# Two widening layers formed by features instead of by tokens, in a two-block transformer kernel

## Chip, core and metric

The kernel runs as one program on one core of a Trainium2 chip. The metric is the device time of one execution in microseconds (us), the median of three runs. Smaller is better. The engines are named as the profile names them: PE is the matrix engine, PEld its weight loads, DVE the vector engine, ACT the scalar engine, POOL the general-purpose engine, SP the queue that issues the large loads.

## The reference, cut to what matters

Two transformer blocks run one after the other on 256 tokens of width 2048, all in float32. The parts that the change touches are the feed-forward networks at the end of each block:

```python
# end of the first block, D_FF = 8192
u = jax.nn.relu(rms_norm(h, mlp_norm_g) @ w_up)
h = h + (u * u) @ w_down
...
# end of the second block, D_FF_2 = 5632
h = rms_norm_2(x, ln_ffn_pre[l])
y = (jax.nn.silu(h @ w_gate[l]) * (h @ w_up[l])) @ w_down[l]
x = x + rms_norm_2(y, ln_ffn_post[l])
```

`rms_norm` divides each token by its root mean square and multiplies by a gain per feature. The widening layers are `w_up` (2048 to 8192) in the first network, `w_gate` and `w_up` (2048 to 5632) in the second.

## The kernel before

**Products in split form.** Each float32 operand is held as a high part, rounded to the type fp32r, and a low part, the rest. A product is three matmuls: high by high, high by low, low by high. Weights come from memory in units of 128 x 1024 floats (two k tiles of 512 columns); ACT writes the high part (`wh`, line 133 by way of line 360), DVE the low part (`wl`, line 366). Five raw buffers and six pairs of `wh` and `wl` are in rotation, and a unit is split up to four units ahead of its use.

**Groups.** `run_groups` (lines 399 to 481) walks a list of groups, each a product of the 256 tokens with 512 output columns. For each k tile of 128 rows it takes the tokens in two halves `t` of 128. The tokens are the stationary operand (128 columns, loaded into the array before each matmul) and 512 weight columns move past them, so that the result has tokens on the partitions and features along the row. One bank of PSUM holds one half; four banks serve two groups in turn. A group with 16 k tiles issues 96 matmuls of 512 columns (lines 460 to 462), and `up` and gate groups have 16 k tiles. A form with the weights stationary and 256 tokens moving exists for the two narrow weights of 20 and 48 columns alone (`swap`, lines 447 to 456).

**What follows a group.** When a group's last matmul is written, its `done` generator becomes a task. `pump` steps the tasks between k tiles, so that their matmuls, transposes and evacuations are placed into the queues between the matmuls of the next groups. The order on every engine is thus written out ahead of time; on the chip an instruction waits only for semaphores and for the one before it on its engine. A planner's clocks (`pe_t`, `act_t`, `dve_t`) decide at which k tile a step is placed.

**The widening layers.** In the first network `up` (line 1065) takes one of 16 groups: ACT applies relu and the token's reciprocal root mean square (`rs`, one number per partition) to each bank, DVE squares the result, and `u_T` transposes it by eight 128 x 128 transposes on PE (line 203, two lots of four) and splits it into high and low parts with ACT and DVE, because the narrowing product needs the features on the partitions. In the second network `ffn_gate` (line 1625) and `ffn_up` (line 1634) do the same for 11 pairs of groups with silu and a product; the eight transposes follow each `ffn_up`. The narrowing groups (`dn`, `fd`) follow two widening groups later, so that `up2` and `up3` come before `dn0_0`.

**The norm.** The gain is applied to the tokens' transposed tiles; the sums of squares are formed by ACT, reduced by DVE, raised to the power -0.5 by POOL (`rstd`, line 232), and the result scales the outputs. In the first network this chain runs in the task of the group `out3`, just as `up0` begins; in the second network it runs during `fg0`.

Of the kernel before, what the change touches and what calls it, by code (L numbers as in the profile page):

```python
# [10 lines left out]
F32 = mybir.dt.float32  # L11
# [79 lines left out]
class Group:  # L91
    def __init__(self, name, w, lhs, done, need=None, n=512, fine=False):
        self.name, self.lhs, self.done, self.need, self.n = name, lhs, done, need or {}, n
        self.bk = {}
        self.task = self.tset = self.tneed = None
        self.per_t = self.resume = self.pause = False
        self.swap = n < 512
        if n == 512:
            srcs = []
            for c in range(w.shape[0]):  # L100
                d = 1 if fine and c == 0 else 2
                srcs += [(w[c][:, j:j + d, :], d, 4 * c + j) for j in range(0, 4, d)]
        else:
            srcs = [(w, 16, 0)]
        self.units = [Unit(self, s, k, n, kt0, i == 0, i == len(srcs) - 1)
                      for i, (s, k, kt0) in enumerate(srcs)]


class Program:
# [289 lines left out]
    def run_groups(self, groups):  # L399
# [27 lines left out]
        for un, ts, ahead in steps:  # L427
            g = un.grp
            if un.first and not g.resume:
                for t in ts:  # L430
                    g.bk[t] = self.bank()
            while self.si < un.i:
                self.split(self.si + 1)
            self.ahead = ahead
            self.more()
            for e in g.need.get(un.kt0 // 4, ()):
                self.need(e if g.tneed is None else (*e, ts[0]))
            lhs = g.lhs()
            h, l = un.pair
            n = un.n  # L440
            self.pe_t = max(self.pe_t, un.ready)
            for k in range(un.nkt):
                kt = un.kt0 + k
                H, L = lhs[0][kt // 4], lhs[1][kt // 4]
                st, sp = un.first and k == 0 and not g.resume, un.last and k == un.nkt - 1 and not g.pause
                wh, wl = h[:, k * n:k * n + n], l[:, k * n:k * n + n]
                if g.swap:
                    c = (kt % 4) * 256
                    o = g.bk[0]["ap"][:n, :256]
                    mm(o, wh, H[:, c:c + 256], start=st, stop=False)  # L450
                    mm(o, wl, H[:, c:c + 256], start=False, stop=False)  # L451
                    mm(o, wh, L[:, c:c + 256], start=False, stop=sp)  # L452
                    self.pe_t += 325.0
                    if k % 4 == 3 and not sp:
                        self.pump()
                    continue
                for t in ts:
                    c = (kt % 4) * 256 + t * 128
                    o = g.bk[t]["ap"]
                    mm(o, H[:, c:c + 128], wh, start=st, stop=False)  # L460
                    mm(o, H[:, c:c + 128], wl, start=False, stop=False)  # L461
                    mm(o, L[:, c:c + 128], wh, start=False, stop=sp)  # L462
                    self.pe_t += 648.0
                if sp:
                    break
                if len(ts) == 2 or k % 2:
                    self.pump()
            if 1 in ts:
                if un.slot is None:
                    self.R.put(*un.pair)  # L470
                else:
                    self.pfree[un.slot] = self.pe_t
                    self.ring.append(un.slot)
            if un.last and not g.pause:
                if g.per_t:
                    self.over(g, g.done(g.bk[ts[0]]["ap"], ts[0]), [g.bk[ts[0]]])
                elif 1 in ts:
                    bs = [g.bk[t] for t in sorted(g.bk)]
                    self.over(g, g.done([b["ap"] for b in bs]), bs)
                self.pump()  # L480
# [96 lines left out]
    def fin_ssq(self, sq, key):  # L577
        s2 = self.stat(2)
        self.red(s2, sq, OP.add)
        self.rs[key] = self.rstd(s2, 2, 2048.0)  # L580
        self.ev.add(("rs", key))

    def free_TT(self, key):
        for x in self.TT.pop(key):
# [3 lines left out]
def v3(f, a):  # L588
    return f.rearrange("p (a b) -> p a b", a=a)


class Kernel(Program):
# [470 lines left out]
        yield from self.norm_T(f, c, "h", "mlp_norm_g", self.sq_h)  # L1063

    def up(self, banks, j):
        yield from self.until(("rs", "h"))
        rs = self.rs["h"]
        (f,) = yield from self.F.wait()
        f3 = v3(f, 2)
        for t in range(2):  # L1070
            self.act(f3[:, t], banks[t], AF.Relu, scale=rs[:, t:t + 1])
        if j == 15:
            self.free_TT("h")
        yield "B"
        self.tt(f, f, f, OP.mult)
        yield 1
        yield from self.u_T(f3, j, 2)
        self.F.put(f)

    def u_T(self, f3, j, per):  # L1080
        h, l = yield from self.R.wait(2)
        yield from self.T_split(f3, None, h, l)
        H, L = self.TT.setdefault(("u", j // per), ([None] * per, [None] * per))
        H[j % per], L[j % per] = h, l
        self.ev.add(("u", j))

    def down(self, banks, b, c):
# [546 lines left out]
    def ffn_up(self, banks, j):  # L1634
# [13 lines left out]
        H[k], L[k] = h, l  # L1648
        self.ev.add(("w", j))

    def ffn_down(self, banks, b, c):
        if b == 0:
            (f,) = yield from self.F.wait()
            self.S["y", c] = f
            for t in range(2):
                self.copy(v3(f, 2)[:, t], banks[t])
            yield "B"
        else:
            f = self.S["y", c]
            f3 = v3(f, 2)  # L1660
            for t in range(2):
                self.tt(f3[:, t], banks[t], f3[:, t], OP.add)
            yield "B"
        if c == 3:
            self.free_TT(("w", b))
# [92 lines left out]

    def build(self):
        nc, A = self.nc, self.A  # L1760
        self.rs, self.S, self.nsq = {}, {}, {}
        self.TT = {"o": ([None] * 4, [None] * 4), "a": ([], []), "p": ([], [])}
        self.gla_e = self.gla_n = 0
        self.KEEP = 6
# [89 lines left out]
        for c in range(4):  # L1854
            G.append(g("out%d" % c, A["w_out"][c], "o", lambda b, c=c: self.wout(b, c), L("oT")))

        ups = [g("up%d" % j, A["w_up"][j], "h", lambda b, j=j: self.up(b, j), L("h") if j == 0 else None)
               for j in range(16)]

        def downs(b):  # L1860
# [4 lines left out]
        def inter(up, dn, nb, per):  # L1865
# [3 lines left out]
                seq += dn(b)  # L1869
            return seq  # L1870

        mlp = inter(lambda b: ups[2 * b:2 * b + 2], downs, 8, 2)
        G += mlp

# [60 lines left out]
        def gu(b):  # L1935
            r = []
            for j in range(2 * b, min(2 * b + 2, 11)):
                r.append(g("fg%d" % j, A["w_gate"][j], "hf", lambda k, j=j: self.ffn_gate(k, j),
                           L("hf") if j == 0 else None))
                r.append(g("fu%d" % j, A["w_up_2"][j], "hf", lambda k, j=j: self.ffn_up(k, j)))  # L1940
            return r

        def fd(b):
# [4 lines left out]

        ffn = inter(gu, fd, 6, 2)
        ffn[0].tset, ffn[0].tneed = "fg0", True  # L1950
        for x in ffn[-4:]:
            x.tset, x.per_t = "fd5", True
        G += ffn
# [193 lines left out]
```

## Time and profile before

| what | value |
|---|---|
| median of three runs | 2643.56 us (2643.45 to 2644.34) |
| profiled execution's own time | 2642.02 us |
| its span, first to last instruction | 2640.3 us |
| PE busy | 2616.5 us (99% of the span), 12196 matmuls |
| PEld busy | 2168.9 us (82%) |
| DVE busy | 1504.9 us (57%) |
| ACT busy | 1251.9 us (47%) |
| POOL busy | 76.5 us (3%) |
| granted PE clock, mean | 0.998 of full speed |
| loads of weights | 473.16 MB on the SP queue |

Busy time of a group of instructions is the union of their durations. A matmul's recorded duration is longer than the distance from its start to the next one's start, since matmuls are pipelined; the speed of a stream is read from starts. The three large groups of the page are the matmuls of lines 460, 461 and 462, each 3496 times, and the chain that ended last runs for 94% of the span through PE.

### The profile page before, as it was taken

How to read it: one execution, taken by the hardware profiler on the slowest of the kernel's cores; microseconds unless marked ns; L12 is line 12 of the kernel's file. 1: busy time of each engine (PE TensorE's matmuls, PEld its weight loads, DVE VectorE, ACT ScalarE, POOL GpSimd, SP SyncE). 2: the span in 40 equal slices, each digit the busy share in tenths (PEclk: the TensorE clock that was granted, in tenths of full speed). 3: DMA queues.
4: the chain of work that ended last, by engine and by line, in shares of the span. 5: the costliest groups of instructions: out<-in, count | busy, mean ns of one | idle time of the engine just before them, and what ended most of it. 6: DMA issues, size and time to landing. Idle time of an engine off the chain costs nothing.

```text
span 2640.3 us, 32053 instructions
## 1 busy us (share of the span) xinstructions
PE 2616.5 (99%) x12196; PEld 2168.9 (82%) x12196; DVE 1504.9 (57%) x1921; ACT 1251.9 (47%) x1708; POOL 76.5 (3%) x97
## 2 busy tenths in 40 slices
PE   9999999999999999999999999999999999999998
PEld 7888888888888888888888888888788888888886
DVE  6567655555555555555566545666755455555555
ACT  7544544444444444444455344465554444444443
POOL 0001000000000000001000000000100000000001
PEclk9999999999999999999999999999999999999999
DMA  9643565555566565555444557555455555556553
GB/s 343 204 139 119 166 216 185 188 188 184 191 201 223 187 223 195 191 202 198 150 143 147 190 177 258 201 199 184 136 193 189 192 188 194 186 195 202 195 186 129
DMA packets 138891, 500.18 MB, mean 189 GB/s; under 512 B 15650, under 2 KB 16594, under 8 KB 138737
## 3 DMA queue, kind: packets, MB, share of 16 engines
q1 hardware_dynamic: 131760, 473.16, 53.0%
q0 software_dynamic: 6976, 24.98, 2.7%
q8 instruction: 95, 1.56, 0.2%
q14 instruction: 60, 0.48, 0.1%
HBM read 493.33 MB, written 7.88 MB: 190 GB/s over the span
## 4 chain that ended last, share of the span: by engine, by line
PE 94%; issue 4%; DVE 1%; ACT 0%; DMA 0%; POOL 0%; SPq 0%; DVEq 0%; ACTq 0%; POOLq 0%
PE gb L460 29%; PE gb L462 29%; PE gb L461 29%; PE pb L197 4%; PE pb L203 3%; DVE wl L366 0%; DVE s L169 0%; DMA s<-memT 0%; DVE s L158 0%; POOL st L232 0%; ACT wh L133 0%; PE gb L451 0%; ACT s L133 0%; PE gb L450 0%; PE gb L452 0%
## 5 line engine op out<-in xcount | busy, mean ns | idle before, releaser
L366 DVE TENSOR_TENSOR wl<-raw,wh 128x1024 fp32r<-128x1024 f32 (+1 forms) x876 | 1052.8, 1219 | 689.5 <-ACT wh L133 687.4
L460 PE MATMUL gb<-wh,s 128*128 128x512 f32 x3496 | 1383.9, 396 | 2.2 <-ACT wh L133 2.1
L461 PE MATMUL gb<-wl,s 128*128 128x512 f32 x3496 | 1362.5, 390 | 2.5 <-DVE wl L366 2.5
L462 PE MATMUL gb<-wh,s 128*128 128x512 f32 x3496 | 1363.4, 390 | 0.0
L133 ACT ACTIVATE wh<-raw 128x1024 fp32r<-128x1024 f32 (+1 forms) x878 | 914.0, 1055 | 802.2 <-PE gb L462 766.8
L462 PEld LDWEIGHTS gb<-wh,s 128*128 128x128 f32 x3496 | 656.4, 188 | 139.3 <-DVE s L169 0.5
L460 PEld LDWEIGHTS gb<-wh,s 128*128 128x128 f32 x3496 | 657.2, 188 | 137.4 <-ACT wh L133 3.7
L461 PEld LDWEIGHTS gb<-wl,s 128*128 128x128 f32 x3496 | 657.5, 188 | 135.1 <-DVE wl L366 4.2
L158 DVE TENSOR_TENSOR s<-gb,s 128x512 f32<-128x512 f32 x144 | 98.1, 691 | 159.6 <-PE gb L462 130.5
L133 ACT ACTIVATE s<-pb 128x512 fp32r<-128x512 f32 (+4 forms) x171 | 89.4, 536 | 163.6 <-PE pb L203 139.5
L133 ACT ACTIVATE s<-gb,st 128x512 f32<-128x512 f32 (+1 forms) x112 | 70.0, 642 | 199.5 <-PE gb L462 188.0
L197 PE MATMUL pb<-s,s 128*128 128x128 f32 (+4 forms) x720 | 116.5, 301 | 1.3 <-DVE s L158 0.9
L203 PE MATMUL pb<-cc,s 128*128 128x128 f32 x700 | 106.0, 274 | 5.4 <-DVE s L169 5.3
L203 PEld LDWEIGHTS pb<-cc,s 128*128 128x128 f32 x700 | 87.0, 141 | 29.0 <-DVE s L169 6.6
L197 PEld LDWEIGHTS pb<-s,s 128*128 128x128 f32 x720 | 97.7, 191 | 9.5 <-DVE s L158 1.3
L158 DVE TENSOR_TENSOR s<-pb,s 128x512 fp32r<-128x512 f32 (+4 forms) x87 | 57.5, 664 | 62.4 <-ACT s L133 58.6
L133 ACT ACTIVATE s<-pb,vecs 128x256 fp32r<-128x256 f32 (+2 forms) x109 | 42.3, 453 | 49.9 <-PE pb L203 40.5
L163 DVE TENSOR_SCALAR s<-gb,st 128x512 f32<-128x512 f32 (+1 forms) x32 | 20.9, 658 | 67.8 <-PE gb L462 51.5
L169 DVE SCALAR_TENSOR_TENSOR s<-pb,vecs,s 128x256 fp32r<-128x256 f32 (+1 forms) x104 | 40.0, 435 | 29.0 <-ACT s L133 29.0
L133 ACT ACTIVATE s<-s,st 128x128 f32<-128x128 f32 (+2 forms) x73 | 32.8, 450 | 31.7 <-DVE st L163 30.4
L133 ACT ACTIVATE s<-s 128x512 f32<-128x512 f32 (+3 forms) x46 | 37.0, 807 | 21.5 <-DVE s L158 12.4
L232 POOL TENSOR_TENSOR st<-st,nhalf 128x8 f32<-128x8 f32 (+2 forms) x21 | 26.1, 1243 | 689.5 <-DVE st L165 689.5
(113 smaller groups left out, 565.0 us busy)
## 6 DMA issues: line engine op xcount, KB each, us to landing
raw<-w_in SPq DMA_DIRECT2D x216, 512.0 KB, 4.2
raw<-w_up SPq DMA_DIRECT2D x216, 512.0 KB, 4.4
raw<-w_down SPq DMA_DIRECT2D x216, 512.0 KB, 4.4
raw<-w_gate SPq DMA_DIRECT2D x88, 512.0 KB, 4.6
raw<-w_out SPq DMA_DIRECT2D x32, 512.0 KB, 4.5
raw<-w_mix_out SPq DMA_DIRECT2D x32, 512.0 KB, 4.6
raw<-w_br_pool SPq DMA_DIRECT2D x16, 512.0 KB, 5.2
raw<-w_br_attn SPq DMA_DIRECT2D x16, 512.0 KB, 4.1
```

The lines of the kernel that those rows point to most:

```text
L133: self.nc.scalar.activation(out, in_, func, **kw)
L158: self.nc.vector.tensor_tensor(out, a, b, op)
L163: self.nc.vector.tensor_scalar(out, a, s1, None, op0=op0)
L169: self.nc.vector.scalar_tensor_tensor(out, a, s, b, op0, op1)
L197: self.nc.tensor.matmul(out, lhsT, rhs, start=start, stop=stop)
L203: self.nc.tensor.transpose(out, in_, self.ident[:k, :k])
L232: self.nc.gpsimd.tensor_tensor(r, t, self.nhalf[:, :k], op=OP.pow)
L366: self.nc.vector.tensor_sub(l[:, :m], r, h[:, :m].bitcast(F32))
L460: mm(o, H[:, c:c + 128], wh, start=st, stop=False)
L461: mm(o, H[:, c:c + 128], wl, start=False, stop=False)
L462: mm(o, L[:, c:c + 128], wh, start=False, stop=sp)
```

## The change

Each group gets a flag `ft`. Where it is set, the loop takes the 512 weight columns of a k tile as four stationary pieces of 128 columns, and the 256 tokens move past each; two pieces share one bank. The result has features on the partitions and tokens along the row. The flag is set on all 16 `up` groups and on the gate and up groups 1 to 10 of the second network; groups `fg0` and `fu0` stay as they were. The token's scale now lies along the row, so `rows_bc` spreads `rs` over all partitions by two matmuls of a broadcast column with the identity and keeps it in a tile `rb`, once per network. `up`, `ffn_gate_ft` and `ffn_up_ft` multiply by `rb` on DVE, and `split_SB` splits the result straight from SBUF. `u_T` and its transposes are gone.

```diff
--- before.py
+++ after.py
@@ -95,6 +95,7 @@
         self.task = self.tset = self.tneed = None
         self.per_t = self.resume = self.pause = False
         self.swap = n < 512
+        self.ft = False
         if n == 512:
             srcs = []
             for c in range(w.shape[0]):
@@ -454,6 +455,18 @@
                     if k % 4 == 3 and not sp:
                         self.pump()
                     continue
+                if g.ft:
+                    c = (kt % 4) * 256
+                    for j in range(4):
+                        o = g.bk[j // 2]["ap"][:, (j % 2) * 256:(j % 2) * 256 + 256]
+                        for p, (a, b) in enumerate(((wh, H), (wl, H), (wh, L))):
+                            mm(o, a[:, j * 128:j * 128 + 128], b[:, c:c + 256], start=st and j % 2 == 0 and p == 0,
+                               stop=sp and j % 2 == 1 and p == 2, skip_group_check=True)
+                        self.pe_t += 324.0
+                    if sp:
+                        break
+                    self.pump()
+                    continue
                 for t in ts:
                     c = (kt % 4) * 256 + t * 128
                     o = g.bk[t]["ap"]
@@ -580,6 +593,28 @@
         self.rs[key] = self.rstd(s2, 2, 2048.0)
         self.ev.add(("rs", key))
 
+    def rows_bc(self, key):
+
+        yield from self.until(("rs", key))
+        (f,) = yield from self.F.wait()
+
+        def pe(i, b):
+            for t in range(2):
+                self.mm(b[:, t * 128:t * 128 + 128], self.rs[key][:, t:t + 1].to_broadcast([128, 128]),
+                        self.ident, True, True)
+
+        def ev(i, b):
+            for t in range(2):
+                self.vcopy(f[:, t * 256:t * 256 + 256], b[:, :256])
+
+        yield from self.pipe([0], [(pe, [ev])])
+        self.rb[key] = f
+        self.ev.add(("rb", key))
+
+    def split_SB(self, f, h, l):
+        self.act(h, f)
+        self.tt(l, f, h.bitcast(F32), OP.subtract)
+
     def free_TT(self, key):
         for x in self.TT.pop(key):
             self.R.put(*x)
@@ -1063,25 +1098,23 @@
         yield from self.norm_T(f, c, "h", "mlp_norm_g", self.sq_h)
 
     def up(self, banks, j):
-        yield from self.until(("rs", "h"))
-        rs = self.rs["h"]
+        yield from self.until(("rb", "h"))
+        rb = self.rb["h"][:, :512]
         (f,) = yield from self.F.wait()
-        f3 = v3(f, 2)
-        for t in range(2):
-            self.act(f3[:, t], banks[t], AF.Relu, scale=rs[:, t:t + 1])
+        f2 = v3(f, 2)
+        for k in range(2):
+            self.stt(f2[:, k], banks[k], 0.0, rb, OP.max, OP.mult)
         if j == 15:
             self.free_TT("h")
+            self.F.put(self.rb.pop("h"))
         yield "B"
-        self.tt(f, f, f, OP.mult)
+        self.act(f, f, AF.Square)
         yield 1
-        yield from self.u_T(f3, j, 2)
+        h, l = yield from self.R.wait(2)
+        self.split_SB(f, h, l)
         self.F.put(f)
-
-    def u_T(self, f3, j, per):
-        h, l = yield from self.R.wait(2)
-        yield from self.T_split(f3, None, h, l)
-        H, L = self.TT.setdefault(("u", j // per), ([None] * per, [None] * per))
-        H[j % per], L[j % per] = h, l
+        H, L = self.TT.setdefault(("u", j // 2), ([None] * 2, [None] * 2))
+        H[j % 2], L[j % 2] = h, l
         self.ev.add(("u", j))
 
     def down(self, banks, b, c):
@@ -1648,6 +1681,36 @@
         H[k], L[k] = h, l
         self.ev.add(("w", j))
 
+    def ffn_gate_ft(self, banks, j):
+        yield from self.until(("rb", "hf"))
+        (f,) = yield from self.F.wait()
+        for k in range(2):
+            self.tt(v3(f, 2)[:, k], banks[k], self.rb["hf"][:, :512], OP.mult)
+        yield "B"
+        self.act(f, f, AF.Silu)
+        yield 1
+        for k in range(2):
+            self.tt(v3(f, 2)[:, k], v3(f, 2)[:, k], self.rb["hf"][:, :512], OP.mult)
+        self.S["g", j] = f
+        self.ev.add(("g", j))
+
+    def ffn_up_ft(self, banks, j):
+        yield from self.until(("g", j))
+        f = self.S.pop(("g", j))
+        for k in range(2):
+            self.tt(v3(f, 2)[:, k], banks[k], v3(f, 2)[:, k], OP.mult)
+        if j == 10:
+            self.free_TT("hf")
+            self.F.put(self.rb.pop("hf"))
+        yield "B"
+        h, l = yield from self.R.wait(2)
+        self.split_SB(f, h, l)
+        self.F.put(f)
+        b, k, n = j // 2, j % 2, 2 if j < 10 else 1
+        H, L = self.TT.setdefault(("w", b), ([None] * n, [None] * n))
+        H[k], L[k] = h, l
+        self.ev.add(("w", j))
+
     def ffn_down(self, banks, b, c):
         if b == 0:
             (f,) = yield from self.F.wait()
@@ -1758,7 +1821,7 @@
 
     def build(self):
         nc, A = self.nc, self.A
-        self.rs, self.S, self.nsq = {}, {}, {}
+        self.rs, self.rb, self.S, self.nsq = {}, {}, {}, {}
         self.TT = {"o": ([None] * 4, [None] * 4), "a": ([], []), "p": ([], [])}
         self.gla_e = self.gla_n = 0
         self.KEEP = 6
@@ -1854,7 +1917,11 @@
         for c in range(4):
             G.append(g("out%d" % c, A["w_out"][c], "o", lambda b, c=c: self.wout(b, c), L("oT")))
 
-        ups = [g("up%d" % j, A["w_up"][j], "h", lambda b, j=j: self.up(b, j), L("h") if j == 0 else None)
+        def ft(x):
+            x.ft = True
+            return x
+
+        ups = [ft(g("up%d" % j, A["w_up"][j], "h", lambda b, j=j: self.up(b, j), L("h") if j == 0 else None))
                for j in range(16)]
 
         def downs(b):
@@ -1869,6 +1936,13 @@
                 seq += dn(b)
             return seq
 
+        for x in G[-4:]:
+            if x.name == "out3":
+                old = x.done
+                def out3(b):
+                    sp(self.rows_bc("h"), "rows h")
+                    yield from old(b)
+                x.done = out3
         mlp = inter(lambda b: ups[2 * b:2 * b + 2], downs, 8, 2)
         G += mlp
 
@@ -1935,9 +2009,12 @@
         def gu(b):
             r = []
             for j in range(2 * b, min(2 * b + 2, 11)):
-                r.append(g("fg%d" % j, A["w_gate"][j], "hf", lambda k, j=j: self.ffn_gate(k, j),
-                           L("hf") if j == 0 else None))
-                r.append(g("fu%d" % j, A["w_up_2"][j], "hf", lambda k, j=j: self.ffn_up(k, j)))
+                if j == 0:
+                    r.append(g("fg0", A["w_gate"][0], "hf", lambda k: self.ffn_gate(k, 0), L("hf")))
+                    r.append(g("fu0", A["w_up_2"][0], "hf", lambda k: self.ffn_up(k, 0)))
+                    continue
+                r.append(ft(g("fg%d" % j, A["w_gate"][j], "hf", lambda k, j=j: self.ffn_gate_ft(k, j))))
+                r.append(ft(g("fu%d" % j, A["w_up_2"][j], "hf", lambda k, j=j: self.ffn_up_ft(k, j))))
             return r
 
         def fd(b):
@@ -1948,6 +2025,11 @@
 
         ffn = inter(gu, fd, 6, 2)
         ffn[0].tset, ffn[0].tneed = "fg0", True
+        fu0 = ffn[1].done
+        def with_rows(b):
+            sp(self.rows_bc("hf"), "rows hf")
+            yield from fu0(b)
+        ffn[1].done = with_rows
         for x in ffn[-4:]:
             x.tset, x.per_t = "fd5", True
         G += ffn
```

## Rows read from the trace of the kernel before

**Rows 1.** The page: busy time of PE, chain that ended last.

```profile
PE 2616.5 (99%) x12196; PEld 2168.9 (82%) x12196; DVE 1504.9 (57%) x1921; ACT 1251.9 (47%) x1708; POOL 76.5 (3%) x97
...
PE 94%; issue 4%; DVE 1%; ACT 0%; DMA 0%; POOL 0%; SPq 0%; DVEq 0%; ACTq 0%; POOLq 0%
```

**Rows 2.** Busy time by stretch (from:to, length, engines, clock, DMA): groups up4 and up5.

```profile
608.24:630.00 21.76, 21.76 (x98) 18.02 (x96) 10.51 (x10) 7.91 (x8) 0.00 (x0) 1.00 0.58 192
630.00:652.70 22.70, 22.70 (x106) 18.81 (x104) 12.05 (x11) 10.60 (x13) 0.00 (x0) 1.00 0.55 189
```

**Rows 3.** Line 203 (transposes), 473 to 1142 us, then 1945 to 2608 us.

```profile
L203 PE MATMUL pb<-cc,s x136: 270/272/273, 478.4 to 1105.9; 128*128 128x128 f32 x136
...
L203 PE MATMUL pb<-cc,s x88: 270/272/273, 1947.5 to 2568.3; 128*128 128x128 f32 x88
```

**Rows 4.** Timeline of PE (start us, us, line, form): 20 weight columns stationary.

```profile
99.74 0.28 PE L450 MATMUL gb<-s,wh 128*20 128x256 f32 x1
...
100.67 0.28 PE L452 MATMUL gb<-s,wh 128*20 128x256 f32 x1
...
101.01 0.28 PE L452 MATMUL gb<-s,wh 128*20 128x256 f32 x1
...
102.37 0.28 PE L452 MATMUL gb<-s,wh 128*20 128x256 f32 x1
```

**Rows 5.** Timeline of PE: 128 columns stationary, 256 moving; first, last of eight runs.

```profile
1369.40 0.52 PE L197 MATMUL pb<-s,s 128*128 128x256 f32 x3
1369.76 0.40 PE L460 MATMUL gb<-wh,s 128*128 128x512 f32 x1
...
1439.81 0.52 PE L197 MATMUL pb<-s,s 128*128 128x256 f32 x3
1440.16 0.40 PE L460 MATMUL gb<-wh,s 128*128 128x512 f32 x1
```

**Rows 6.** Timeline of PEld: ten weight loads in a row between 64-column matmuls.

```profile
1368.28 1.20 PEld L197 LDWEIGHTS pb<-s,s 128*128 128x128 f32 x10
```

**Rows 7.** Groups by line and form, weight loads (count, busy us, mean ns).

```profile
L461 PEld LDWEIGHTS gb<-wl,s 128*128 128x128 f32 x3496 | 657.5, 188 | 135.1 <-DVE wl L366 4.2 <-issue 1.0
...
L451 PEld LDWEIGHTS gb<-s,wl 128*48 128x48 f32 x16 | 1.9, 122 | 0.1
...
L451 PEld LDWEIGHTS gb<-s,wl 128*20 128x20 f32 x16 | 1.6, 98 | 0.4
```

**Rows 8.** Timeline of PE after 256-column matmuls: the first 512-column ones.

```profile
1275.70 0.40 PE L460 MATMUL gb<-wh,s 128*128 128x512 f32 x1
...
1276.86 0.39 PE L462 MATMUL gb<-wh,s 128*128 128x512 f32 x1
```

**Rows 9.** POOL and PE in group up0: the norm's power, the third k tile.

```profile
475.36 0.72 POOL L232 TENSOR_TENSOR st<-st,nhalf 128x2 f32<-128x2 f32 x1 [148.30 <-DVE st L165]
...
475.70 0.39 PE L460 MATMUL gb<-wh,s 128*128 128x512 f32 x1
```

**Rows 10.** Timeline of PE: eight passes of plain float32 matmuls.

```profile
310.91 1.05 PE L197 MATMUL pb<-s,s 128*128 128x128 f32 x8
```

**Rows 11.** Groups by line and form: evacuations in both networks, wide ACT copies.

```profile
L133 ACT ACTIVATE s<-gb,st 128x512 f32<-128x512 f32 x32 | 21.9, 690 | 56.6 <-PE gb L462 56.6
L133 ACT ACTIVATE s<-pb 128x512 fp32r<-128x512 f32 x32 | 19.2, 600 | 53.2 <-PE pb L203 53.2
...
L158 DVE TENSOR_TENSOR s<-s 128x1024 f32<-128x1024 f32 x16 | 19.5, 1219 | 0.0
...
L158 DVE TENSOR_TENSOR s<-gb,s 128x512 f32<-128x512 f32 x31 | 21.3, 692 | 38.1 <-PE gb L462 38.1
L169 DVE SCALAR_TENSOR_TENSOR s<-gb,st,s 128x512 f32<-128x512 f32 x22 | 15.7, 751 | 26.9 <-PE gb L462 26.9
...
L133 ACT ACTIVATE s<-s 128x1024 f32<-128x1024 f32 x18 | 19.0, 1054 | 15.3 <-DVE s L169 9.0 <-DVE s L158 6.2
```

**Rows 12.** Busy time by stretch: the second network from fg1 to its last pair.

```profile
1944.78:2607.92 663.14, 663.14 (x2969) 549.25 (x2968) 339.55 (x318) 278.34 (x286) 4.91 (x4) 1.00 0.58 191
```

## The prediction

> **What bounds the kernel now.** I read the page first. PE is busy for 99% of the span, and the chain that ended last runs through PE for 94% of it [rows 1]. So time is won only by taking work off PE, and lost only by giving it more, or by making it wait. Next I read busy time by stretch, one group to a stretch. A widening group without transposes, up4, takes 21.76 us, and PE has no idle time in it; up5, in which the eight transposes of up4's result are placed, takes 22.70 us [rows 2]. The granted clock is 1.00 in both, the upper of the two levels (2.4 GHz). Both lengths recur through the networks, so they are countable pieces. 21.76 us over 96 matmuls is 0.2267 us for one of 512 columns. A set of eight transposes costs 22.70 - 21.76 = 0.94 us, all of it on the path.
>
> The sum is made against the profiled execution's 2642.02 us, 1.7 us over its span. The median of the runs, 2643.56 us, is 1.5 us above it, and I add that at the end.
>
> **Transposes that go.** From 473 to 1142 us there are 136, which is 17 sets; one belongs to out3's norm and stays, so 16 go. From 1945 to 2608 us there are 88, 11 sets; the set of fu0 stays, so 10 go [rows 3]. 26 x 0.94 = 24.4 us. The evacuations that went with them are off PE and dealt with below.
>
> **The matmuls themselves.** 36 groups of 96 matmuls with 512 columns become 36 groups of 192 with 256 columns: 3456 x 0.2267 = 783.4 us now, and 6912 steps afterwards. Each step now needs its own load of 128 weight columns, twice as many loads as before. The question is how long one step is. At exactly half, 0.1133 us, this part costs nothing; each nanosecond above that costs 6.9 us.
>
> The lower bound comes from the narrow weights, the one place that already keeps weights still and moves 256 tokens. With 20 columns stationary, twelve steps from 101.01 to 102.37 us take 0.1133 us each [rows 4]. That is exactly half of 0.2267, so I see no reason for a gain below it. The run's first eight steps, after the change from 512 columns, took 0.116 (0.93 over 8).
>
> The upper bound comes from the same form as the new one: 128 columns stationary, 256 moving. It occurs in eight short runs of three usable steps each, right behind other work. The first takes 0.36 / 3 = 0.120 us a step and the last 0.35 / 3 = 0.117 [rows 5]; I use 0.119. That would add 6912 x 0.0057 = 39 us (0.1190 - 0.1133).
>
> Which one? By form rows 5 are nearer, but they show only the first three steps of a run, and there the 20-column run is slow as well. Matmuls of 512 columns are also slow when they follow another form: five steps from 1275.70 to 1276.86 us take 0.232 instead of 0.2267 [rows 8]. So I read the 0.119 as a settling after a change of form, not as the price of 128 columns. The second check is the load. Between matmuls that move only 64 columns, ten loads of 128 columns take 1.20 us, the last one recorded 0.19: (1.20 - 0.19) / 9 = 0.112 us a load [rows 6]. That is under 0.1133, if by only 1 ns. A load starts when the matmul before it starts, so load and matmul run side by side and the longer one counts. I take 0.1133 and keep 0.119 as the upper end.
>
> The Trainium skill has a rule here that would change the sum: "TensorE: Matmul & The Clock Gate", section "Wait — 56ns, not 53.3ns?", gives each warm matmul a fixed cost of about 2.5 ns beside its columns. By that rule 3456 more matmuls would cost an estimated 8.6 us. Rows 2 and 4 show 226.7 and 113.3 ns, a ratio of two with nothing fixed left, so this trace does not agree, and the sum goes without it.
>
> **Changes of form.** Every passage between 256 and 512 columns costs the settling: 1.16 - 5 x 0.2267 = 0.027 us [rows 8]. The widening groups come in runs, seven in the first network and five in the second, so there are 24 passages: 0.6 us.
>
> **rows_bc.** Twice, two plain float32 matmuls of 128 columns, four passes each: eight passes recorded at 1.05 us, of which the last one's own length runs beside the next matmul, so about 0.9 us [rows 10], and 0.1 for the passage back: 1.0 us. In the first network the step may also wait. It is placed as soon as out3's norm has been written, which by the planner's clocks is before the third k tile of up0; PE reaches that at 475.70 us, while POOL's power ends at 475.36 + 0.72 = 476.08 [rows 9]. PE's queue is in order, so all of up0's later matmuls stand behind that wait: 0.4 us and a signal, 0.5 in all. Between 0 (placed one k tile later) and 1.9 (one earlier). In the second network rs is long done when fu0 ends, and nothing waits. Together 2.5 us.
>
> **Evacuations, hidden.** For one `up`, ACT did 2 x 690 + 2 x 600 = 2580 ns and now does two passes of 1024 at 1054: 2108. DVE did 1219 + 2 x 692 = 2603 and now does 2 x 751 + 1219 = 2721. For one pair of the second network, ACT falls likewise; DVE did 2 x 751 + 2 x 692 = 2886 and now does six passes of 692 and one of 1219: 5371 [rows 11], 2.5 us more, 24.8 us for ten pairs. From fg1 to the last pair DVE is busy for 339.6 of 663.1 us [rows 12], so 25 us more lie in 323 us of idle time. A bank is needed again only two groups later, and weights are split up to four units ahead, 4 x 2.72 = 10.9 us; that is the cover. The narrowing groups come two groups after the results they need, so the last of them is no more late than now. No DMA is added or moved, and the SP queue is passed by nothing new; its loads follow the release of the raw buffers, which follows PE.
>
> **Sum.** -24.4 + 0 + 0.6 + 2.5 = -21.3 us: 2620.7 for a profiled execution, 2622.2 us for the median.
>
> **The rivals.**
>
> A, slower: the weight loads are the bound. With two ends only 1 ns apart (0.112 for a load, 0.1133 for a matmul), any slip of the load delays the next matmul, nothing is ever caught up, and the steps stay at rows 5's 0.119. Place: PEld, in all 36 groups. Price: 39 us, so 2622.2 + 39 = 2661 us. It decides the sign from 21.3 / 6.912 = 3.1 ns, a step of 0.1164 us. For it: these are the only rows of the very form, and all eight runs agree. Against it: they are beginnings, and loads of 20 columns begin nearly as slowly.
>
> B, between: the streams settle but slip again at each new unit of weights, every 24 matmuls. The whole run of 20 columns from 99.74 to 102.37 us is 23 steps at 0.1143 with its settling inside [rows 4]; at that mean the price is 6.9 us: 2629. For it: each unit begins with waits for ACT and DVE. Against it: groups of 512 columns keep 0.2267 over eight units.
>
> C, much slower: a load occupies PE for its whole recorded time. That is 98 ns for 20 columns, 122 for 48, 188 for 128 [rows 7], so 6912 x 0.188 = 1299 us in place of 783: 3138 us. The Trainium skill speaks for it: the same page, in "Part 3: Packing small matmuls — row/col tiling" under "What overlaps and what doesn't", says that weight loads overlap running matmuls only when they use another group of rows, which these do not. This trace does not agree: 188 ns of load and 512 columns fit into 0.2267 us, and rows 5 hold steps of 0.12 us with loads of 128 columns between.
>
> D, same time: DVE's 24.8 us of new work in the second network come at the wrong moments (three products, then the split of the next weights late, then PE waiting for `wl`). If all of it showed, 2647 us. Against it: rows 12.
>
> That the change does not do what it says can only mean transposes left over; the diff keeps one set, and that is counted.
>
> **How the numbers follow.** The forecast has 0.52 (2619 to 2627), B 0.13, A 0.26 (2650 to 2675 around 2661), D 0.05, C 0.02, and 0.02 lies between. A measurement can tell 0.2%, 5.3 us, from no change. Faster: the forecast and B, 0.65. Same: D and the rest between, 0.07. Slower: A and C, 0.28. The range goes from 2619, the full saving with the wait in `rows_bc` gone and some error, to 2664, which takes in the upper end of the step; it leaves out some of A, C and a little below, 0.18. As cases of both signs hold the chances, the likeliest one's own range is 2619 to 2627.
>
> **What would show it.** Right: widening groups of 21.8 us as stretches, up4 and up5 alike, 208 transposes gone from line 203, PE without idle time in the networks, and PE starts 0.1133 apart after the first few. If a widening group takes 22.9 us (192 x 0.119), A holds; 21.95, B; gaps on PE released by DVE `wl` in the second network, D. Ahead of the third k tile of up0 there should be a gap of about half a microsecond on PE, released by POOL. The prediction is wrong if the step stays above 0.1164 us.

## The result, and the profile after

The changed kernel takes 2665.94 us (median of 4 runs, 2664.56 to 2667.04) against 2643.95 us for the kernel before in the same session (4 runs, 2643.45 to 2646.07). The ratio is 1.0081 with a 95% interval of 1.0064 to 1.0099: slower by 22 us. The forecast was 2622.2 us, faster. The profiled execution took 2666.71 us, 24.7 us more than the one before the change.

The page of the changed kernel, first busy time, the chain that ended last, and three of its costliest groups (answers to [rows 1]; lines are shifted, the new matmuls are line 463):

```profile
PE 2641.2 (99%) x15452; PEld 2332.1 (88%) x15452; DVE 1530.8 (57%) x1955; ACT 1243.9 (47%) x1656; POOL 76.6 (3%) x97
...
PE 86%; issue 11%; DVE 1%; ACT 0%; POOL 0%; DMA 0%; SPq 0%; DVEq 0%; ACTq 0%; POOLq 0%
...
L463 PE MATMUL gb<-s,wh 128*128 128x256 f32 x4608 | 832.6, 283 | 0.0
L463 PEld LDWEIGHTS gb<-s,wh 128*128 128x128 f32 x4608 | 720.5, 192 | 0.4
L463 PE MATMUL gb<-s,wl 128*128 128x256 f32 x2304 | 652.7, 283 | 0.0
```

PE is still busy for 99%, and the new matmuls have no idle time ahead of them (the last column). In the chain PE falls from 94 to 86% and "issue", which names no engine and no wait, rises from 4 to 11%. PE's busy time rose by 24.7 us, as much as the whole. So the time did not go into waits; PE itself needs longer. The stretches say where (columns as in [rows 2]): up4, up5, and the narrowing group behind them.

```profile
611.45:634.48 23.03, 23.03 (x193) 23.03 (x192) 11.02 (x11) 8.47 (x8) 1.54 (x3) 1.00 0.56 186
634.48:657.52 23.04, 23.04 (x194) 23.04 (x193) 12.13 (x12) 10.25 (x10) 0.00 (x0) 1.00 0.52 184
657.52:668.43 10.91, 10.91 (x51) 9.03 (x49) 7.20 (x8) 6.03 (x6) 0.00 (x0) 1.00 0.53 176
```

In [rows 2] up4 was 21.76 and up5 22.70 us. Now both are 23.04: the 0.94 us of transposes is gone from up5, and each of the two has 1.28 us more. A step is the distance from one matmul's start to the next one's: 23.04 us over 192 matmuls is 120.0 ns a step, and every step behind the first two is 119 to 121. 34 of the 36 groups are so; the other two, up0 and fg1, also hold other work of PE. The granted clock is 1.00, as before. 36 x 1.28 = 46.1 us is more than the 24.4 us that the transposes gave back.

Line 204 (203 before) over the whole run, its matmuls on PE:

```profile
L204 PE MATMUL pb<-cc,s x492: 212/272/475, 73.1 to 1956.9; 128*128 128x128 f32 x163, 20*128 20x20 f32 x1
```

492 against 700 before: 208 transposes are gone, as counted from [rows 3].

The wait that was forecast ahead of up0's third k tile, first PE, then POOL (answers to [rows 9]):

```profile
476.81 0.28 PE L463 MATMUL gb<-s,wh 128*128 128x256 f32 x1
477.22 0.71 PE L198 MATMUL pb<-cc,st 128*128 128x128 f32 x4
477.68 0.36 PE L463 MATMUL gb<-s,wh 128*128 128x256 f32 x1
477.88 0.28 PE L463 MATMUL gb<-s,wl 128*128 128x256 f32 x1
```

```profile
476.45 0.71 POOL L233 TENSOR_TENSOR st<-st,nhalf 128x2 f32<-128x2 f32 x1 [148.30 <-DVE st L166]
```

The step after 476.81 would have begun at 476.93; PE stood until POOL's 477.16 and a signal, 0.29 us. But `rows_bc` has four passes on record, not eight (the prediction counted four for each of its two matmuls, the trace has two), so up0 is longer by 0.74 us in all (24.72 = 0.94 + 23.04 + 0.74). In the second network the whole step costs 0.36 us, the first stretch below (fu0) against 21.76; the second stretch, from fg1 to the end of the narrowing groups fd4, holds the same work as [rows 12]:

```profile
1931.04:1953.16 22.12, 22.12 (x101) 18.39 (x100) 12.18 (x12) 12.01 (x13) 0.00 (x0) 1.00 0.75 260
...
1953.16:2632.50 679.34, 679.34 (x4811) 641.93 (x4810) 363.51 (x349) 275.81 (x266) 4.82 (x4) 1.00 0.54 187
```

DVE's busy time rose there from 339.55 to 363.51 us, by 24.0, and PE is busy in all 679.34 us: DVE's new work is hidden.

The account: matmuls +46.1, transposes -24.4, `rows_bc` +0.74 + 0.36, twelve passages to a narrowing group at 0.03 (10.91 against 10.88 us) +0.4, and 1.1 us that are lost before the changed code begins (both kernels' first large matmul starts at 6.42 us, their 97th at 32.58 and 33.64 us). That is 24.3 of the 24.7 us between the two profiled executions.

### The profile page after: what moved, and what is told of

Read it like the earlier page. It is cut to its first block, busy times and chain, and to the rows that moved or that the text cites. A ratio compares the mean times of both kernels' runs of the same rounds, so it can differ in the third digit from the quotient of the medians.

```text
span 2664.9 us, 38579 instructions
## 1 busy us (share of the span) xinstructions
PE 2641.2 (99%) x15452; PEld 2332.1 (88%) x15452; DVE 1530.8 (57%) x1955; ACT 1243.9 (47%) x1656; POOL 76.6 (3%) x97
## 4 chain that ended last, share of the span: by engine, by line
PE 86%; issue 11%; DVE 1%; ACT 0%; POOL 0%; DMA 0%; SPq 0%; DVEq 0%; ACTq 0%; POOLq 0%
PE gb L463 31%; PE gb L473 16%; PE gb L474 16%; PE gb L475 16%; PE pb L198 4%; PE pb L204 1%; DVE wl L367 0%; DVE s L170 0%; POOL st L233 0%; DVE s L159 0%; DMA s<-memT 0%; ACT wh L134 0%; ACT s L134 0%; PE gb L451 0%; PE gb L453 0%
## 5 line engine op out<-in xcount | busy, mean ns | idle before, releaser
L473 PE MATMUL gb<-wh,s 128*128 128x512 f32 x2344 | 932.1, 398 | 2.0 <-ACT wh L134 1.8
L474 PE MATMUL gb<-wl,s 128*128 128x512 f32 x2344 | 915.4, 391 | 2.5 <-DVE wl L367 2.5
L475 PE MATMUL gb<-wh,s 128*128 128x512 f32 x2344 | 915.9, 391 | 0.0
L463 PE MATMUL gb<-s,wh 128*128 128x256 f32 x4608 | 832.6, 283 | 0.0
L463 PEld LDWEIGHTS gb<-s,wh 128*128 128x128 f32 x4608 | 720.5, 192 | 0.4
L463 PE MATMUL gb<-s,wl 128*128 128x256 f32 x2304 | 652.7, 283 | 0.0
L473 PEld LDWEIGHTS gb<-wh,s 128*128 128x128 f32 x2344 | 441.6, 188 | 93.5 <-ACT wh L134 3.5
L475 PEld LDWEIGHTS gb<-wh,s 128*128 128x128 f32 x2344 | 440.8, 188 | 94.0 <-DVE s L170 0.5
L474 PEld LDWEIGHTS gb<-wl,s 128*128 128x128 f32 x2344 | 441.7, 188 | 91.4 <-DVE wl L367 4.3
L463 PEld LDWEIGHTS gb<-s,wl 128*128 128x128 f32 x2304 | 442.8, 192 | 0.4
L134 ACT ACTIVATE s<-s 128x1024 f32<-128x1024 f32 (+3 forms) x98 | 91.9, 939 | 113.2 <-DVE s L159 63.3
L159 DVE TENSOR_TENSOR s<-s,s 128x512 f32<-128x512 f32 (+5 forms) x142 | 85.6, 637 | 0.6
```

Of the source, the lines that this page charges most:

```text
L134: self.nc.scalar.activation(out, in_, func, **kw)
L159: self.nc.vector.tensor_tensor(out, a, b, op)
L463: mm(o, a[:, j * 128:j * 128 + 128], b[:, c:c + 256], start=st and j % 2 == 0 and p == 0, stop=sp and j % 2 == 1 and p == 2, skip_group_ch ...
```

## The experiments

The question was why a step of 256 columns takes 120.0 ns and not half of 226.7. In the expectations, theory L is a sharper form of the prediction's rival A: the weight load sets the step, it takes 120 ns for 128 columns, and its length goes with the columns loaded. Theory F: a matmul with a full load costs 6.7 ns beyond its columns' share of 226.7, whatever else it has. Theory S was formed after the first four runs, W after eight. Runs e1, e2, e8 and e9 edit the loop of lines 459 to 465 in the changed kernel; each group's first k tile keeps the old sizes. The kernel before took 2644.34 us beside the first four (median of 8 runs), 2644.02 beside the next four (one run) and 2643.6 beside the last two (median of 13). A time below without a number of runs is of a single run, and what is read there is the steps in its trace, not the total. Stretches below are pairs of widening groups (up4 with up5; fg10 with fu10), 24 steps of 120.0 ns and 360 of the edited kind.

**e1_cols**: fewer columns loaded.

```diff
+W = 128 if kt == 0 else 124 if g.name[:2] == "up" else 112
-mm(o, a[:, j * 128:j * 128 + 128], b[:, c:c + 256], ...
+mm(o, a[:, j * 128:j * 128 + W], b[:, c:c + 256], ...
```

> The changed kernel, but from the second k tile on fewer weight columns are kept stationary: 124 of 128 in the first network, 112 of 128 in the second (the features left out are not computed, so the result is incomplete). Theory L, the load sets the step: a step of the narrow form is the longer of the moving time, 0.1133 us for 256 columns, and the load, 0.120 us for 128 columns and 0.00083 us less for each column left out. It expects 0.1167 us a step and 22.4 us a group in the first network, 0.1133 and 21.8 us in the second, about 2632 us in all. Theory F, the form sets the step: each matmul of 256 columns with a full-height load carries 6.7 ns that do not depend on the columns loaded. It expects 0.120 us a step and 23.04 us a group in both networks, 2666 us.

Measured: 2642.8 us. Stretches, first network and second:

```profile
611.02:657.07 46.05, 46.05 (x385) 46.05 (x384) 23.17 (x22) 18.75 (x18) 1.55 (x3) 1.00 0.56 186
2521.48:2565.15 43.67, 43.67 (x385) 43.67 (x384) 23.19 (x23) 17.93 (x17) 0.00 (x0) 1.00 0.59 193
```

(46.05 - 2.88) / 360 = 119.9 ns with 124 columns, 113.3 with 112 (113.5 from the starts over the whole network). Each theory is right in one network and wrong in the other.

**e2_moving**: other numbers of columns moved, 384 and 192 (`N = 256 if kt == 0 else 384 if g.name[:2] == "up" else 192`, used for the moving operand and the output).

> The changed kernel, but from the second k tile on other numbers of columns move past each load of 128: 384 in the first network, 192 in the second (the extra columns belong to the next k tile or are left out, so the result is not the network's). Theory L (the longer of 0.4427 ns per moving column and 0.120 us for the load): 0.170 us a step and 32.0 us a group in the first network, 0.120 (no less than 0.112) and 23.0 us in the second, about 2810 us. Theory F (6.7 ns on top of each step): 0.1767 us a step and 33.2 us a group in the first network, 0.0917 and 17.9 us in the second, about 2727 us.

Measured: 2789.8 us.

```profile
649.34:714.61 65.27, 65.27 (x386) 65.27 (x384) 23.34 (x22) 18.78 (x18) 1.54 (x3) 1.00 0.39 131
2669.08:2712.13 43.05, 43.05 (x386) 43.05 (x384) 23.16 (x23) 17.94 (x17) 0.00 (x0) 1.00 0.60 196
```

The steps are (65.27 - 2.88) / 360 = 173.3 ns for 384 columns (173.4 from the starts) and 111.6 for 192. Neither theory has these numbers. L falls with the second: full loads can follow one another at 111.6 ns, so it is not their rate alone that sets 120.0. Together with 226.7 and 120.0 the first gives theory S. At the upper clock level, 2.4 GHz, 512, 384 and 256 columns take 213.3, 160.0 and 106.7 ns; the steps are 13.3, 13.4 and 13.3 ns longer. So a step is its columns at 2.4 GHz plus a fixed 13.3 ns, and never less than the 111.6 ns of its load, which agrees with the 0.112 of [rows 6].

**e3_old_form**: the changed kernel with the flag off (`x.ft = True` to `x.ft = False`): tokens stationary again, but still no transposes; the evacuations of the new form run on results in the old layout.

> The changed kernel with the flag ft off: tokens stationary and 512 weight columns moving as before, but the evacuations of the changed kernel and no transposes (so the narrowing layers get their operand in the wrong orientation). It prices the part that was to be won by itself. If the 26 sets of transposes were on the path at 0.94 us and the new evacuations are hidden: widening groups of 21.76 us, 24.4 us less and about 1 us for rows_bc, 2621 us. If the new evacuations or rows_bc cost PE time of their own, correspondingly more, up to 2644 us. Theories L and F expect the same here: all of the loss lies in the step of the narrow form.

Measured: 2620.42 us (4 runs, 2619.55 to 2621.5), ratio 0.9908 (0.9892 to 0.9925). up4 and up5:

```profile
606.58:628.34 21.76, 21.76 (x97) 18.02 (x96) 11.00 (x11) 8.49 (x8) 1.55 (x3) 1.00 0.62 198
628.34:650.10 21.76, 21.76 (x97) 18.02 (x96) 12.13 (x12) 10.27 (x10) 0.00 (x0) 1.00 0.59 192
```

Without the changed matmul form the sum of the other terms holds: 2620.4 against a forecast of 2622.2. So the loss lies in the step of the matmul; what else was missized (`rows_bc`, the changes of form) is small.

**e5_wide**: could the fixed part be paid less often? H and L of a k tile lie side by side, `wh` moves both as one matmul of 512 columns, and `wl` moves H alone: two matmuls a piece instead of three. The two halves overlap in their banks.

```diff
+mm(g.bk[j // 2]["ap"], wh[:, j * 128:j * 128 + 128], HL, ...
+mm(o, wl[:, j * 128:j * 128 + 128], H, ...
```

> The changed kernel, with the tokens' high and low parts side by side in SBUF, so that one matmul moves both (512 columns) past the high part of the weights; the low part of the weights still meets 256 columns. Two loads per piece instead of three. Both halves of the wide product go to separate places of a bank here and overlap those of the neighbour piece, so the sum is not the network's; it is a look at the time. Theory L: the load behind the 512-column matmul is hidden, the other one sets 0.120: 0.2267 + 0.120 = 0.3467 us a piece, 22.2 us a group, about 2637 us, 0.3% faster than the kernel before. The rival, that a passage between 256 and 512 columns costs 0.027 us as after the narrow weights, expects at least 0.027 more per piece: 23.9 us a group and 2695 us.

Measured: 2654.38 us (5 runs, 2652.81 to 2656.28), ratio 1.0037 (1.0024 to 1.0050). PE, timeline in the second network:

```profile
2049.70 0.40 PE L466 MATMUL gb<-s,wh 128*128 128x512 f32 x1
2049.93 0.28 PE L468 MATMUL gb<-s,wl 128*128 128x256 f32 x1
...
2050.76 0.40 PE L466 MATMUL gb<-s,wh 128*128 128x512 f32 x1
```

Three pairs take 1.06 us, 353 ns each: 236.4 for the wide matmul and 117.0 for the narrow one from all starts. L's sum of 346.7, which is S's too, is 6.7 ns short; the rival's 373 or more is 20 ns over. A wide matmul right behind a narrow one is slower than in a run of its kind, as in [rows 8].

**e4_order**: the three products outermost, the four pieces inside, in the order 0, 2, 1, 3, so that no two matmuls in a row write to the same place in PSUM.

> The changed kernel with its twelve matmuls of a k tile in another order: high by high for all four pieces, then low by high, then high by low, so that neighbours write different banks. New theory S, from the first four runs: a step with a load of 128 columns is the moving columns at 2.4 GHz plus a fixed 13.3 ns (512: 226.7, 384: 173.3, 256: 120.0), plus 6.7 ns where fewer columns are loaded (112: 113.3), and no less than the load's own 111.7. It expects 0.120 us a step and 23.04 us a group, as in the changed kernel, 2666 us. The rival, that three matmuls in a row into the same place of PSUM cost the extra 6.7 ns, expects 0.1133 and 21.8 us, 2620 us.

Measured: 2667.34 us; up4 and up5 are 46.07 us long as in the changed kernel:

```profile
612.54:658.61 46.07, 46.07 (x385) 46.06 (x384) 22.55 (x21) 18.72 (x18) 1.54 (x3) 1.00 0.56 186
```

That matmuls in a row write to the same place is not the cause.

**e6_tokens**: the kernel before with, in the first network, 112 of 128 token columns loaded under 512 moving, and in the second 320 of 512 weight columns moving under full loads.

```diff
+if not st and g.name[:2] in ("up", "dn"): W = 112
+if not st and g.name[:2] in ("fg", "fu", "fd") and g.name != "fg": N = 320
```

> The kernel before (tokens stationary), with parts of the work left out from each group's second k tile on: in the first network's up and dn groups 112 of 128 token columns are loaded and 512 columns move, in the second network's gate, up and down groups 128 are loaded and 320 of 512 columns move. Theory S, fixed time per matmul that depends on the columns loaded: 213.3 + 6.7 = 220.0 ns a step in the first network (21.1 us a group of 96 instead of 21.76), 133.3 + 13.3 = 146.7 ns in the second, about 2395 us if the loads from memory keep up. The reading of the prediction, a time per column moved (0.4427 ns) and nothing fixed, expects 226.7 ns in the first network and 141.7 in the second, about 2398 us; the times of the steps tell them apart, not the total.

Measured: 2427.62 us. First up4, then two matmuls 23 steps apart in the second network:

```profile
610.27:632.23 21.96, 21.96 (x98) 16.82 (x97) 10.52 (x10) 7.91 (x8) 0.00 (x0) 1.00 0.61 196
```

```profile
2047.70 0.31 PE L465 MATMUL gb<-wh,s 128*128 128x320 f32 x1
...
2051.07 0.31 PE L467 MATMUL gb<-wh,s 128*128 128x320 f32 x1
```

3.37 / 23 = 146.5 ns for 320 columns (146.6 over all): S's 146.7, not the 141.7 of a proportional step. In the first network S expected 220.0 and missed: up4 takes 21.96 us, not less than the 21.76 with full loads. The total is 33 us above the 2395 that S expected, most of it from these steps. So 112 loaded columns instead of 128 shorten a step of 256, not one of 512.

**e8_cols2**: as e1, with 120 and 116 columns.

> The changed kernel with 120 (first network) and 116 (second) of 128 weight columns loaded from the second k tile on; 124 cost as much as 128 and 112 cost 6.7 ns less. If the load counts in pieces of 16 columns, both take 0.120 us a step and about 2666 us. If it counts in pieces of 8, 120 columns take less than 0.120 in the first network and 116 as much as 120. Theory L in its first form (0.00083 us less for each column left out) expected 0.1133 in both and about 2622 us; the run with 124 columns already speaks against it.

Measured: 2645.65 us.

```profile
607.76:652.86 45.10, 45.10 (x385) 45.09 (x384) 23.15 (x22) 18.75 (x18) 1.55 (x3) 1.00 0.57 189
2523.14:2568.01 44.87, 44.87 (x386) 44.87 (x384) 23.23 (x23) 17.94 (x17) 0.00 (x0) 1.00 0.57 189
```

(45.10 - 2.88) / 360 = 117.3 ns and (44.87 - 2.88) / 360 = 116.6 ns. Between 124 columns (119.9) and 112 (113.3) the step falls by degrees. Pieces of 16 are refuted, as 120 columns take less than 128. Pieces of 8 come close (124 as much as 128, and 120 and 116 within 0.7 ns of each other), but no run settles them.

**e9_moving2**: as e2, with 240 and 224 columns moving.

> The changed kernel with 240 (first network) and 224 (second) columns moving past 128 loaded ones, from the second k tile on. Theory S with its floor: 100.0 + 13.3 = 113.3 ns a step in the first network; in the second 93.3 + 13.3 = 106.7 is under the load's own time, so 111.7. That is 21.8 us and 21.5 us a group, about 2617 us. If the load alone set the step (theory L), both stay at 0.120 us. If only the moving columns did (0.4427 each and 6.7 more), 112.9 and 105.8.

Measured: 2612.86 us.

```profile
604.23:647.41 43.18, 43.18 (x385) 43.17 (x384) 23.09 (x22) 18.75 (x18) 1.54 (x3) 1.00 0.60 197
2492.14:2535.20 43.06, 43.06 (x385) 43.05 (x384) 23.17 (x23) 17.94 (x17) 0.00 (x0) 1.00 0.60 194
```

The steps are 111.9 and 111.6 ns, against S's 113.3 and 111.7. L's 120.0 is refuted a second time. 16 columns fewer took 8 ns off where S gives 6.7, so S is not exact next to the load's 111.6. The third number of each line is PEld's busy time: all of the stretch, as in the changed kernel, though the loads go 8 ns faster here. A load's record (192 ns) is not what it occupies, and a PEld that looks full is no sign of the bound.

**e7_halves**: the kernel before, tokens stationary and transposes kept, with the 512 weight columns of its widening groups moved in two halves. Theory W: freshly written weights as the loaded operand cost the 13.3 ns.

```diff
+for q in (slice(0, 256), slice(256, 512)):
+    for p, (a, b) in enumerate(((H, wh), (H, wl), (L, wh))):
+        mm(o[:, q], a[:, c:c + 128], b[:, q], ...
```

> The kernel before (tokens stationary, transposes kept), with one edit: in the up groups and in fg/fu 1 to 10 the 512 weight columns of a k tile move as two halves of 256, so each group has 192 matmuls of 256 columns with the 128 token columns stationary. The loaded tiles are the old ones (token tiles, written long before); nothing of the evacuations or of rows_bc is new. Theory S (a step is columns/2.4 GHz plus 13.3 ns, whichever operand is loaded): steps of 120.0 ns, widening groups of 23.04 us plus 0.94 us where eight transposes lie in them, and 36 x 1.28 = 46 us more than before: 2690 us. Rival W (what costs the 13.3 ns is that the loaded tiles are freshly written weights, or the features' form): steps of 113.3 ns, groups of 21.76 us, 2644 us.

Measured: 2689.23 us. The pair up4 and up5 with one set of transposes:

```profile
614.43:661.36 46.93, 46.93 (x393) 46.93 (x392) 22.57 (x21) 18.53 (x20) 0.00 (x0) 1.00 0.55 180
```

46.93 = 2 x 23.04 + 0.85. Only the number of columns that a matmul moves was changed here, and with it the number of matmuls and of their loads, and it costs 45.6 us. W is refuted: weights or tokens as the loaded operand, the step is 120.0 ns.

**e10_wide1**: e5's form in the first network alone, the second as before, and the four wide matmuls of a k tile in a row, then the four narrow ones, so that the form changes less often.

> First network only, second as in the kernel before: the weights stationary, and high x [H|L] moved as one matmul of 512 columns for four pieces of a k tile, then the four low x H of 256 columns; the products of the two halves overlap in their banks, so the network's sums are not the reference's. The first k tile of a group goes in the narrow form. Theory S with no cost for a change of form: a k tile takes 4 x 226.7 + 4 x 120.0 = 1387 ns, a group 15 x 1.387 + 1.44 = 22.2 us without transposes against 21.76 + 0.94 = 22.70 before: 16 x 0.5 = 8 us less and about 1 us for rows_bc, 2637 us. Rival (each change between 256 and 512 columns costs what the first rows of such a stretch show, 0.027 us, two per k tile): 1441 ns, a group of 23.0 us, 2650 us.

Measured: 2641.65 us (10 runs, 2640.42 to 2643.21) against 2643.6 (13 runs), ratio 0.9993 (0.9984 to 1.0003): no difference that can be told. Two groups, then PE's order:

```profile
607.76:652.72 44.96, 44.96 (x265) 39.65 (x264) 22.51 (x22) 18.75 (x18) 1.55 (x3) 1.00 0.61 191
```

```profile
640.09 1.09 PE L466 MATMUL gb<-s,wh 128*128 128x512 f32 x4
641.02 0.63 PE L475 MATMUL gb<-s,wl 128*128 128x256 f32 x4
641.49 0.87 PE L466 MATMUL gb<-s,wh 128*128 128x512 f32 x3
```

A k tile takes 0.93 + 0.47 = 1.40 us, a group 22.48. S alone gave 1387 ns, the rival 1441; the four wide matmuls behind narrow ones take about 232 ns each, not 226.7, and the narrow ones 118.5, so a k tile has some 16 ns over S's sum where the rival has 54. Per pair of groups that is 0.44 us less than 2 x 21.76 and two sets of transposes; by an estimate, 8 x 0.44 us less 0.74 for `rows_bc` is 2.8 us, 0.1% of the kernel, and to give the network's sums the form would need more banks and DVE work, which no run has. No version here that does all the work of the kernel before is faster than it.

## Why the prediction was wrong

**The step that failed** is "At exactly half, 0.1133 us, this part costs nothing", with the choice "I take 0.1133 and keep 0.119 as the upper end". The step is 120.0 ns, the term +46.1 us instead of 0, and that alone turns the sign: with 46.1 in its place the sum is -21.3 + 46.1, +24.8 us, and +24.7 was measured (with 1.1 us from ahead of the changed code, and `rows_bc` 1.4 us cheaper).

The 0.1133 came from a stationary operand of 20 columns [rows 4], the 226.7 it was compared with from one of 128. "A ratio of two with nothing fixed left" was read from two different forms. At 2.4 GHz, 512 columns are 213.3 ns and 256 are 106.7: the wide step holds 13.3 ns beside its columns, the 20-column step 6.7. Both parts stand in rows 2 and 4, and taking the columns' time at the granted clock off each step, instead of dividing one step by the other, would have shown them. The second check, a load of 0.112 us under a matmul of 0.1133 and "the longer one counts", failed as well: the measured step is longer than both. For the new form, 128 columns loaded and 256 moving, the right figure was rows 5's 0.119: the nearest rows by form were explained away as settling. Runs e2, e6 and e7 show in their place: columns / 2.4 GHz + 13.3 ns for full loads at 256 and more moving columns. This is a fit to the steps of 256, 320, 384 and 512 columns; what the 13.3 ns are made of is open.

The rule of the Trainium skill that the prediction set aside, "TensorE: Matmul & The Clock Gate", section "Wait — 56ns, not 53.3ns?", was right in kind: a warm matmul has a fixed cost beside its columns. Its size, about 2.5 ns there, is 13.3 ns for this kernel's matmuls of 256 to 512 columns.

**Rival A** had the step (0.119) and nearly the time (2661) right; its mechanism is half refuted. The rate of the loads was not the bound: full loads go at 111.6 ns under 192 and 224 moving columns (e2, e9), as [rows 6] had said, and slips between two ends 1 ns apart cannot give the same 13.3 ns at 384 and 320 moving columns (e2, e6), where a step is far longer than a load. At 256 columns, though, the load has a part: with 112 columns loaded the step falls to 113.3 ns (e1), the prediction's own value, and with 240 moving to 111.9 (e9), the load's. The changed kernel's own trace says so too (PE, where up4 begins, first, second and fifth matmul):

```profile
611.45 0.28 PE L463 MATMUL gb<-s,wh 128*128 128x256 f32 x1
611.56 0.28 PE L463 MATMUL gb<-s,wl 128*128 128x256 f32 x1
...
611.92 0.28 PE L463 MATMUL gb<-s,wl 128*128 128x256 f32 x1
```

The first step behind a 512-column matmul takes 112 to 114 ns in all eleven such passages, the later ones 0.12 us: a run of 256 columns starts at the fast step and settles at the slow one, the other way round than the prediction read rows 5. So about half of the 13.3 ns at 256 columns may still be A's slip; no run here decides it.

**Right:** the transposes' 24.4 us (e3), the evacuations hidden, which refutes D (DVE +24.0 us for 24.8 forecast, PE busy throughout), and POOL's wait in up0 by its place. **Too large:** `rows_bc`, 2.5 us forecast, 1.1 measured, mainly since eight passes were counted and four ran; the changes of form, 0.6 forecast, 0.4 measured, as only the 12 passages to a narrowing group cost anything. **B** (slips at each unit) is refuted: in a group without other work every step behind the first two is 119 to 121 ns, across its units. **C** (a load occupies its recorded 188 ns) is refuted by steps of 120.0 with loads recorded at 192; the rule of the Trainium skill cited for it, the same page's "What overlaps and what doesn't", does not hold for these matmuls.

Open: whether the 13.3 ns belong to the matmul or to the load that each one has, as every matmul in every run here has a load of its own (the page counts 15452 of each); why fewer loaded columns take up to 6.7 ns off a step of 256 (e1, e8) and nothing off one of 512 (e6); why 240 columns are 1.4 ns faster than S gives (e9); and why a wide matmul is slow behind narrow ones (e5, e10).

## What to carry to other kernels

Before a matmul is cut into narrower ones, take its columns' time at the granted clock off its step: what is left is paid once per matmul with its load, and again for every such pair that is added. Here it is 13.3 ns, so 96 more matmuls a group cost 1.28 us, and eight transposes of 0.94 us per one or two groups were the cheaper way. A price from a row that differs from the new form in one operand's size is at best a bound, and a row of the very form, even a short one, weighs more.

## Unexpected of the hardware

A matmul's step does not scale with its moving columns: 226.7 ns for 512, 173.4 for 384, 146.6 for 320, 120.0 for 256, then 111.9, 111.6 and 111.6 for 240, 224 and 192, where the load of 128 columns seems to set it (ten loads in a row took 0.112 us each, [rows 6]). At 256 moving columns the step also depends on how many columns are loaded: 120.0 for 128, 119.9 for 124, 117.3 for 120, 116.6 for 116, 113.3 for 112, and 113.3 for 20 [rows 4].
